# Hybrid encoder block: TensorE's matmuls in the order in which the program traces them

## The chip, the cores and the metric

One core of a Trainium2 chip runs the kernel. The metric is the device time of one execution in microseconds; the time of a kernel is the median of its runs. A separate execution was profiled, and all rows below come from it.

## The reference

One layer on x of 256 tokens by 2048 channels, float32, and a final RMSNorm. Cut to what matters:

```python
def hybrid_layer(x, ...):
    h = rms_norm(x, norm1_g)
    u_a, v_a, feat_b, gate_a, gate_b = split_cols(h @ w_in, ...)
    y_a = sgu_mixer(u_a, v_a, ...)       # gelu, layer norm over channels, 128x128 mix of positions
    y_b = rwkv_mixer(feat_b, ...)        # 16 heads of 64, forward and backward state scans
    merged = sigmoid(gate_a) * (y_a @ w_proj_a) + sigmoid(gate_b) * (y_b @ w_proj_b)
    x = x + merged @ w_out
    h2 = rms_norm(x, norm2_g)
    gt = dwconv3_centred(h2 @ ffn_w_gate, ffn_conv_w, ffn_conv_b)
    return x + (silu(gt) * (h2 @ ffn_w_up)) @ ffn_w_down
```

All weights and activations are float32; w_in has 9,632 columns, the ConvGLU 5,632.

## The kernel before

**Large products.** Every weight column block of 128 is a *job* (`push`, line 196), and its 2048 rows come in *chunks* of four 128x128 blocks. A chunk is loaded by SP (`raw`), split into a high and a low part by a cast on ScalarE (line 271) and a subtraction on VectorE (line 272), and used by TensorE in `advance` (line 276): for each block one matmul of 512 columns with the high part against both parts of the activation (line 294), and one of 256 columns with the low part (line 298). So a chunk has eight matmuls, four pairs. `hl`, the split tiles, has four buffers, and three chunks are split ahead (`HL_AHEAD`). A job's sums are evicted by ScalarE (line 310) and VectorE (line 311). The w_down product at the end uses `tok_mm` (lines 230 to 232).

**Small work between the chunks.** The spatial gating unit (`sgu`, line 470) and the RWKV mixer are Python generators. `run` (line 368) takes a step of a generator, then calls `advance` for as many chunks as the yielded number is worth, and so on. In `sgu` the sum over channels of v is a matmul of `ones` with `acc` (lines 472 and 484), into the PSUM tile ms; then come rsqrt, a transpose (line 497, sgt) and the mix (line 503, sgm).

The RWKV mixer works on eight head pairs p. A round of the loop in line 1011 runs `rwkv_chain(p)` (state steps over four blocks of 64 tokens; matmuls into cc and oc) abreast of `rwkv_inverse(p + 1)` (gp: lines 770 and 782; tp: lines 808 to 859), with `rwkv_rates(p + 2)`. Then, in a second `run`, `rwkv_norm(p)` alternates with `rwkv_operands(p + 2)`. I call this second part the end of the round. Its matmuls all write the pool `ps_ms`, which has one buffer:

- `head_sums` (line 642): two matmuls with `bones`, for the high and the low part `bs` that `split` makes on ScalarE (line 184) and VectorE (line 185);
- the transposes of v (line 731), read by eight ScalarE copies into UV and ZR (lines 739 and 740);
- in `rwkv_norm` the bones of O, read by line 949; the bones of O squared (line 952), read by line 959; and the four g matmuls (lines 965 to 968);
- in `rwkv_operands` the bones of hs (lines 745 and 746), read by line 751.

Round p=-1 has only the inverse of head pair 0; ahead of it the rates and operands of pair 0 run alone. From round p=5 on fewer chunks are left to place between the steps, and round p=6 has no operands, p=7 neither operands nor inverse.

After the rounds come the products with w_pb (activation ybs, after a load sab of spilled gates), w_out (activation mg), the second norm (lines 1099 to 1112) and the ConvGLU.

**The order.** The program is traced in Python order, and a scheduler then orders each engine's queue: an instruction that by its cost table is not ready lets later ones of the same engine pass. So the order on TensorE is not the one in which `advance` and the generators wrote it.

```python
    def head_sums(b):
        ps = ps_ms.tile([P, 512], F32, name="ms", tag="ms")
        for o in range(2):
            PE.matmul(ps[:, 0:T], bones, b[:, o], start=(o == 0), stop=(o == 1))
        return ps[:, 0:T]
```

Of the kernel before, what the change touches and what calls it, by code (L numbers as in the profile page):

```python
# [119 lines left out]
    return out  # L120


@with_exitstack
def hybrid_kernel(ctx: ExitStack, tc: tile.TileContext, xT, w_in, w_pa, w_pb, w_out, w_g, w_u, w_d,
                  cols, consts, lora, sgu_wT, sgu_b, norm_f, out):
    nc = tc.nc
    V, A, PE, G = nc.vector, nc.scalar, nc.tensor, nc.gpsimd

    cpool = ctx.enter_context(tc.tile_pool(name="cpool", bufs=1))
    ps_mm = ctx.enter_context(tc.tile_pool(name="ps_mm", bufs=2, space=PSUM))  # L130
# [880 lines left out]
    for p in range(-1, NP):  # L1011
# [15 lines left out]
        n = left() - (LAST if p == NP - 1 else 0)  # L1027
# [252 lines left out]
```

## Time and profile before

| | us |
|---|---|
| median of three runs | 1546.63 (1545.62 to 1550.25) |
| the profiled execution | 1550.3 |
| its span, first to last instruction | 1548.2 |
| PE busy | 1525.0 (99%) |
| DVE busy | 1214.3 (78%) |
| ACT busy | 925.0 (60%) |
| POOL busy | 38.1 (2%) |

PE is TensorE, DVE VectorE, ACT ScalarE, POOL GpSimd. The 274.65 MB of DMA traffic make 177 GB/s over the span. A matmul's end in the profile is modelled, and matmuls are pipelined, so the distance between the starts of two matmuls says more than their durations.

### The profile page before, as it was taken

The page shows a single profiled execution, that of the slowest core. Times are in us where ns is not written, and L with a number is a line of the kernel's source. Part 1 is how long each engine was busy: PE and PEld are TensorE (multiplying, and loading weights), DVE is VectorE, ACT ScalarE, POOL GpSimd, SP SyncE. Part 2 cuts the span into 40 slices and gives each one's busy share as a digit, 9 for nine tenths or more (in the row PEclk, how much of TensorE's full clock was granted, in tenths as well). Part 3 has the DMA queues.
Part 4 walks back from the last instruction along what each step waited for, and adds up shares of the span by engine and source line. Part 5 has one row for each costly group of instructions (what it writes and reads, how often), then busy time and mean ns, then how long its engine had stood idle before and what let it go on. Part 6 is the DMA issues. An engine that isn't in the chain of part 4 may idle for free.

```text
span 1548.2 us, 34103 instructions
## 1 busy us (share of the span) xinstructions
PE 1525.0 (99%) x12680; PEld 1310.8 (85%) x12680; DVE 1214.3 (78%) x2496; ACT 925.0 (60%) x1946; POOL 38.1 (2%) x63
## 2 busy tenths in 40 slices
PE   9999999999999999989999999999999999999997
PEld 8888888888788878878888888888888888888886
DVE  8979998899889997678778777777777777555544
ACT  7767666665665664556665666665656666544442
POOL 0000000000000000000000000000000000000000
PEclk9999999999999999999999999999999999999999
DMA  8555453443443333587655555555555556766663
GB/s 282 187 176 186 155 165 123 132 133 133 134 141 121 125 100 129 178 272 244 207 189 183 189 191 190 190 189 192 190 190 188 192 188 217 230 193 194 194 175 110
DMA packets 148165, 274.65 MB, mean 177 GB/s; under 512 B 17056, under 2 KB 19232, under 8 KB 147872
## 3 DMA queue, kind: packets, MB, share of 16 engines
q1 hardware_dynamic: 145296, 265.14, 52.7%
q0 software_dynamic: 2560, 7.34, 1.5%
q8 instruction: 99, 1.62, 0.4%
q14 instruction: 66, 0.54, 0.1%
q10 hardware_dynamic: 144, 0.01, 0.0%
HBM read 266.13 MB, written 6.29 MB: 176 GB/s over the span
## 4 chain that ended last, share of the span: by engine, by line
PE 83%; issue 9%; DVE 4%; DMA 1%; ACT 1%; POOL 0%; SPq 0%; DVEq 0%; ACTq 0%; POOLq 0%
PE mm L294 40%; PE mm L298 21%; PE pd L232 5%; PE pd L230 5%; PE pd L231 5%; PE gp L770 1%; PE tp L818 1%; DVE hl L272 1%; PE ms L642 1%; DMA sab<-spill 1%; DVE FQ L796 1%; PE tp L808 1%; DMA spill<-ev 1%; PE cc L901 0%; ACT hl L271 0%
## 5 line engine op out<-in xcount | busy, mean ns | idle before, releaser
L294 PE MATMUL mm<-h,hl 128*128 128x512 f32 x2624 | 930.1, 395 | 0.0
L272 DVE TENSOR_TENSOR hl<-raw,hl 128x512 fp32r<-128x512 f32 x960 | 656.7, 691 | 218.9 <-ACT hl L271 215.5
L271 ACT CAST hl<-raw 128x512 fp32r<-128x512 f32 x960 | 593.5, 621 | 380.3 <-PE mm L298 162.8
L298 PE MATMUL mm<-h,hl 128*128 128x256 f32 x2624 | 740.6, 282 | 1.5 <-DVE hl L272 1.3
L294 PEld LDWEIGHTS mm<-h,hl 128*128 128x128 f32 x2624 | 492.8, 188 | 103.8
L298 PEld LDWEIGHTS mm<-h,hl 128*128 128x128 f32 x2624 | 495.9, 189 | 3.0 <-DVE hl L272 2.1
L310 ACT COPY ev<-mm 128x256 f32<-128x256 f32 x196 | 73.1, 373 | 125.2 <-PE mm L298 123.3
L231 PE MATMUL pd<-hl,act 128*128 128x512 f32 x352 | 136.9, 389 | 0.0
L230 PE MATMUL pd<-hl,act 128*128 128x512 f32 x352 | 136.9, 389 | 0.0
L232 PE MATMUL pd<-hl,act 128*128 128x512 f32 x352 | 136.9, 389 | 0.0
L311 DVE TENSOR_TENSOR ev<-mm,ev 128x256 f32<-128x256 f32 x196 | 82.9, 423 | 44.6 <-ACT ev L310 43.2
L294 PE MATMUL mm<-mg,hl 128*128 128x512 f32 x256 | 90.7, 395 | 0.0
L231 PEld LDWEIGHTS pd<-hl,act 128*128 128x128 f32 x352 | 66.1, 188 | 13.8
L232 PEld LDWEIGHTS pd<-hl,act 128*128 128x128 f32 x352 | 66.1, 188 | 13.8
L230 PEld LDWEIGHTS pd<-hl,act 128*128 128x128 f32 x352 | 66.1, 188 | 13.6
L298 PE MATMUL mm<-mg,hl 128*128 128x256 f32 x256 | 72.1, 282 | 0.0
L294 PEld LDWEIGHTS mm<-mg,hl 128*128 128x128 f32 x256 | 48.1, 188 | 9.6
L294 PE MATMUL mm<-ybs,hl 128*128 128x512 f32 x128 | 46.1, 401 | 4.0 <-DVE ev L311 3.4
L298 PEld LDWEIGHTS mm<-mg,hl 128*128 128x128 f32 x256 | 48.4, 189 | 0.0
L294 PE MATMUL mm<-ya,hl 128*128 128x512 f32 x128 | 47.7, 404 | 0.0
L1161 ACT ACTIVATE gt<-cp,colt 128x256 f32<-128x256 f32 x44 | 26.5, 602 | 19.4 <-DVE cp L1159 19.4
L298 PE MATMUL mm<-ybs,hl 128*128 128x256 f32 x128 | 36.8, 287 | 0.0
(292 smaller groups left out, 1430.5 us busy)
## 6 DMA issues: line engine op xcount, KB each, us to landing
raw<-in_w_in_dram SPq DMA_DIRECT2D x304, 256.0 KB, 2.9
raw<-in_w_g_dram SPq DMA_DIRECT2D x176, 256.0 KB, 2.7
raw<-in_w_u_dram SPq DMA_DIRECT2D x176, 256.0 KB, 2.8
raw<-in_w_d_dram SPq DMA_DIRECT2D x176, 256.0 KB, 3.0
raw<-in_w_out_dram SPq DMA_DIRECT2D x64, 256.0 KB, 3.0
raw<-in_w_pa_dram SPq DMA_DIRECT2D x32, 256.0 KB, 2.9
raw<-in_w_pb_dram SPq DMA_DIRECT2D x32, 256.0 KB, 4.3
spill<-ev POOLq DMA_DIRECT2D x32, 128.0 KB, 3.1
```

Of the source, the lines that this page charges most:

```text
L230: PE.matmul(ps, a[:, 0, ts], w[:, 0], start=(k == 0), stop=False)
L231: PE.matmul(ps, a[:, 0, ts], w[:, 1], start=False, stop=False)
L232: PE.matmul(ps, a[:, 1, ts], w[:, 0], start=False, stop=(k == nk - 1))
L271: A.copy(hl[:, 0, :m], raw[:, s0:s0 + m])
L272: V.tensor_tensor(out=hl[:, 1, :m], in0=raw[:, s0:s0 + m], in1=hl[:, 0, :m].bitcast(F32), op=ALU.subtract)
L294: PE.matmul(ps[:, 0:512], hl[:, 0, j], a.rearrange("p a t -> p (a t)"), start=(k == 0), stop=False)
L298: PE.matmul(ps[:, 0:256], hl[:, 1, j], a[:, 0], start=False, stop=(k == job["nk"] - 1))
L310: A.copy(t, ps[:, 256:512])
L311: V.tensor_tensor(out=t, in0=ps[:, 0:256], in1=t, op=ALU.add)
L642: PE.matmul(ps[:, 0:T], bones, b[:, o], start=(o == 0), stop=(o == 1))
L770: PE.matmul(gps[hh][:, c * P:(c + 1) * P], BK[rows, d, c, hh:hh + 2, :].rearrange("p a b -> p (a b)"), AR[rows, d, c].rearrange("p a b -> ...
L1161: A.activation(gt, b[:, 1:T + 1], AF.Identity, scale=col("cw1", f), bias=col("cb", f))
```

## The change

A wrapper stands in for TensorE's engine object. For each matmul and transpose it adds an edge, without a semaphore, from the previous TensorE instruction. The scheduler thus has to keep TensorE's instructions in traced order, and orders the other engines alone.

```diff
+class InOrder:
+    def __init__(self, tc):
+        self.tc, self.last = tc, None
+
+    def _next(self, op, *args, **kw):
+        tc = self.tc
+        traced = tc.nc.cur_bb.bb.instructions
+        n = len(traced)
+        op(*args, **kw)
+        for ins in traced[n:]:
+            if self.last is not None:
+                tc.add_manual_dep(
+                    ins, self.last.name,
+                    mybir.DependencyInfo(mybir.DependencyClass.NoSync, mybir.DependencyReason.DATA),
+                    reason="order")
+            self.last = ins
+
+    def matmul(self, *args, **kw):
+        self._next(self.tc.nc.tensor.matmul, *args, **kw)
+
+    def transpose(self, *args, **kw):
+        self._next(self.tc.nc.tensor.transpose, *args, **kw)
...
-    V, A, PE, G = nc.vector, nc.scalar, nc.tensor, nc.gpsimd
+    V, A, G = nc.vector, nc.scalar, nc.gpsimd
+    PE = InOrder(tc)
```

All TensorE instructions now carry the wrapper's line 133, and other lines of the kernel stand 27 further down.

What moves, first on TensorE at the end of round p=1. The rows name output, inputs and the size of the output; mm is the sum of a chunk's job, h_ its activations. Before, behind the last eviction of the chain (oc):

```order
L932 MATMUL oc<-Gs,UV 64x64 x4
...
L642 MATMUL ms<-bs,bones 128x256
...
L731 MATMUL ms<-cst,vf 128x128 x4
...
L889 MATMUL cc<-ZR,Gs 64x64 x3
L642 MATMUL ms<-bs,bones 128x256
L889 MATMUL cc<-ZR,Gs 64x64
L770 MATMUL gp<-AR_1690,BK 128x128 x2
L642 MATMUL ms<-bs,bones 128x256
L770 MATMUL gp<-AR_1690,BK 128x128 x5
```

and with the change:

```order
L133 MATMUL mm<-h_99,hl 128x256
L133 MATMUL ms<-bs,bones 128x256 x2
L133 MATMUL ms<-cst,vf 128x128 x4
L133 MATMUL mm<-h_100,hl 128x512
...
L133 MATMUL mm<-h_103,hl 128x256
L133 MATMUL ms<-bs,bones 128x256 x2
L133 MATMUL mm<-h_104,hl 128x512
...
L133 MATMUL ms<-bs,bones 128x256 x2
L133 MATMUL ms<-gsp,lg 128x256 x3
...
L133 MATMUL cc<-ZR,Gs 64x64 x4
L133 MATMUL gp<-AR_1690,BK 128x128 x8
```

Before, the two bones matmuls stand apart with two pairs between them, two more pairs stand ahead of the transposes, and the later bones sit inside the cc and gp matmuls of the next round. Now the bones and the transposes follow each other directly, one chunk stands between each of the later steps, and cc and gp are unbroken.

The same on TensorE at the first sum over acc in `sgu`, before:

```order
L298 MATMUL mm<-h_102,hl 128x256
L472 MATMUL ms<-acc,cst 128x256
L294 MATMUL mm<-h_103,hl 128x512
```

and with the change:

```order
L133 MATMUL mm<-h_111,hl 128x256
L133 MATMUL ms<-acc,cst 128x256
L133 MATMUL mm<-h_96,hl 128x512
```

The sum stood behind the seventh pair (h_102) of the job after the last v job; now it stands directly behind the last pair (h_111) of that v job. The first transpose then follows 16 pairs after the second sum, where 23 and a half stood before.

The third place is on TensorE at the operands of head pair 0, before:

```order
L294 MATMUL mm<-ya_131,hl 128x512
L770 MATMUL gp<-AR_1689,BK 128x128 x3
...
L770 MATMUL gp<-AR_1689,BK 128x128 x4
L642 MATMUL ms<-bs,bones 128x256
L770 MATMUL gp<-AR_1689,BK 128x128
```

and with the change:

```order
L133 MATMUL mm<-ya_130,hl 128x256
L133 MATMUL ms<-bs,bones 128x256 x2
L133 MATMUL mm<-ya_131,hl 128x512
...
L133 MATMUL mm<-ya_134,hl 128x256
L133 MATMUL gp<-AR_1689,BK 128x128 x8
```

The bones matmuls were behind seven of the first eight gp matmuls; now they stand behind four pairs of ya, ahead of all gp matmuls. On POOL and SP no row moves; DVE and ACT have the same instructions with some of them in another order.

## Rows read from the trace of the kernel before

**Rows 1.** The page's busy line: us, share of the span, instructions.
```profile
PE 1525.0 (99%) x12680; PEld 1310.8 (85%) x12680; DVE 1214.3 (78%) x2496; ACT 925.0 (60%) x1946; POOL 38.1 (2%) x63
```
**Rows 2.** Timeline of PE, end of round p=1: start us, us, engine, line, operation, count.
```profile
335.25 0.32 PE L642 MATMUL ms<-bs,bones 128*128 128x256 f32 x1
...
336.99 0.64 PE L731 MATMUL ms<-cst,vf 128*128 128x128 f32 x4
...
340.10 0.44 PE L889 MATMUL cc<-ZR,Gs 64*64 64x64 f32 x6
...
343.59 0.40 PE L294 MATMUL mm<-h,hl 128*128 128x512 f32 x1
...
343.94 0.40 PE L294 MATMUL mm<-h,hl 128*128 128x512 f32 x1
```
**Rows 3.** Busy us by stretch: PE, PEld, DVE, ACT, POOL, clock, DMA share, GB/s.
```profile
150.00:663.00 513.00, 505.29 (x7139) 422.71 (x7137) 445.86 (x1022) 316.90 (x764) 23.77 (x44) 1.00 0.42 137
...
684.00:1540.00 856.00, 854.71 (x4616) 743.43 (x4614) 621.38 (x1153) 487.31 (x924) 10.28 (x8) 1.00 0.61 194
```
**Rows 4.** Waits of PE: waiting line, releaser, total us, times, longest us.
```profile
PE mm L294 <- DVE ev L311: 3.4, 1, 3.4
PE tp L808 <- DVE Tc L800: 3.0, 5, 0.9
...
PE gp L770 <- DVE BK L720: 1.1, 1, 1.1
```
**Rows 5.** Timeline of PE, start of round p=0.
```profile
222.59 0.45 PE L889 MATMUL cc<-ZR,Gs 64*64 64x64 f32 x8
222.97 1.16 PE L770 MATMUL gp<-AR,BK 64*128 64x128 f32 x16
224.06 0.50 PE L294 MATMUL mm<-h,hl 128*128 128x512 f32 x1
```
**Rows 6.** Timeline of all engines, first sum over acc.
```profile
54.94 0.42 DVE L415 TENSOR_TENSOR acc<-acc,vu 128x256 f32<-128x256 f32 x1
...
55.42 0.70 PE L472 MATMUL ms<-acc,cst 128*128 128x256 f32 x2
```
**Rows 7.** Timeline of PE, second sum and first transpose in sgu.
```profile
66.07 0.70 PE L484 MATMUL ms<-acc,cst 128*128 128x256 f32 x2
...
74.97 0.44 PE L497 MATMUL sgt<-cst,vu 128*128 128x128 f32 x2
```
**Rows 8.** Timeline of all engines, operands of head pair 0 (in brackets idle time, releaser).
```profile
166.90 0.40 PE L294 MATMUL mm<-ya,hl 128*128 128x512 f32 x1
...
169.77 0.49 PE L770 MATMUL gp<-AR,BK 64*128 64x128 f32 x2 [1.07 <-DVE BK L720]
...
172.36 0.41 ACT L184 CAST bs<-hs 128x256 fp32r<-128x256 f32 x1
...
172.84 0.41 DVE L185 TENSOR_TENSOR bs<-hs,bs 128x256 fp32r<-128x256 f32 x1
```
**Rows 9.** Timeline of DVE and ACT, end of round p=1.
```profile
335.59 0.42 DVE L185 TENSOR_TENSOR bs<-O,bs 128x256 fp32r<-128x256 f32 x1
...
336.49 0.42 DVE L949 SCALAR_TENSOR_TENSOR O<-ms,O 128x256 f32<-128x256 f32 x1
...
336.96 0.62 ACT L271 CAST hl<-raw 128x512 fp32r<-128x512 f32 x1 [1.11 <-PE mm L298]
...
339.63 0.44 ACT L740 COPY ZR<-ms 128x256 f32<-128x256 f32 x1
```
**Rows 10.** Timeline of PE, end of round p=5.
```profile
561.15 0.73 PE L932 MATMUL oc<-Gs,UV 128*64 128x64 f32 x8 [0.23 <-ACT UV L905]
...
562.96 0.34 PE L642 MATMUL ms<-bs,bones 128*128 128x256 f32 x1
```
**Rows 11.** Timeline of PE and ACT, second norm.
```profile
809.59 0.59 PE L1102 MATMUL ms<-tot,cst 128*128 128x256 f32 x2
...
811.12 0.40 ACT L1099 ACTIVATE sqn<-x 128x256 f32<-128x256 f32 x1
```
**Rows 12.** Busy us by stretch, behind the first sab load (columns as in rows 3).
```profile
680.00:683.30 3.30, 3.30 (x11) 2.82 (x12) 2.69 (x7) 1.17 (x3) 0.00 (x0) 0.52 0.69 222
```

## The prediction

> **What bounds the kernel now.** I read the busy line first. TensorE (PE) is busy 1525.0 us of a span of 1548.2, VectorE (DVE) 78% and ScalarE (ACT) 60% [rows 1]. Busy PE time in this profile is partly modelled, so the pace is what counts: one pair, a 512-column matmul (L294) and its 256-column partner (L298), starts every 0.35 us, 343.59 and 343.94 [rows 2]. I call it a pair, and four pairs (one weight chunk, 1.39 us) a chunk. Then the stretches: from 150 to 663 us, where the RWKV rounds run between the chunks, PE is busy 505.29 of 513.00 us, and from 684 to 1540 us 854.71 of 856.00 [rows 3]. The large stall lies between, at the first sab load; no instruction changes places there, so I leave it as it is. Last the list of PE's waits: three lines make up 7.5 us [rows 4]. So PE is the bound nearly everywhere, and the scheduler has already pushed most small matmuls behind enough chunks that their inputs are ready. There is little waiting left to win. The change can win only in the pace, and it can lose by each wait that the pushed-back chunks hid.
>
> **What the change moves.** No instruction is added or removed. PE's order becomes the traced one; SP and POOL keep their order, and DVE and ACT are reordered a little by a scheduler that now sees PE wait. The kernel traces a small matmul right behind the Python step that makes its input, so at these places PE now arrives early.
>
> *Gain: unbroken runs of small matmuls.* In round p=1 of before, cc and gp matmuls alternate with the bones matmuls of `head_sums`. From the first cc to the next chunk it takes 343.59 - 340.10 = 3.49 us [rows 2]. The same cc and gp groups in one piece took 224.06 - 222.59 = 1.47 us [rows 5]. Four bones matmuls of 256 columns in the stream cost a third of a pair each (0.48 together), so 1.54 us went into four interruptions, 0.39 each. The traced order has none. Rounds p=0 to 4 have about four each (in p=0, 2, 4 one of them is gp split by a chunk), and round p=-1 four: 24 x 0.4 = **-9.6 us**.
>
> *Loss 1, SGU.* The first sum over acc (L472) is traced right behind the last chunk of v; before, seven pairs stand ahead of it that now stand behind. PE would come at 55.42 - 7 x 0.345 = 53.0 us, and the last addition to acc ends at 54.94 + 0.42 = 55.36 [rows 6]: a wait of 2.4. From the second sum (66.07) to the first transpose sgt (74.97) it takes 8.9 us through the rsqrt chain [rows 7]; PE now has only 16 pairs in between, 0.34 + 5.5 = 5.9. On DVE and ACT one eviction and one cast leave the path (about 0.9), so I take 2.1. **+4.5 us**, bounds 2.4 and 5.4.
>
> *Loss 2, first operands.* The bones matmuls of p=0 move ahead of gp, after only four pairs of ya: PE comes at 166.90 + 1.4 = 168.3. Their two input halves start on ACT at 172.36 and on DVE at 172.84 [rows 8]. One eviction less stands ahead on each, so I take 172.2 and 172.7 for the matmuls: 3.9 + 0.4 of waiting, against the 1.07 that PE waits there before [rows 4, 8]. **+3.2 us**; the bounds are 1.5 (two split tiles leave the path) and 4.2 (nothing does).
>
> *Loss 3, the end of each round,* where `rwkv_norm` and the next `rwkv_operands` alternate on the single ms buffer. I go through p=1, with one chunk between steps. (a) bones: the second half comes from DVE at 335.59 + 0.42 = 336.01, so the second bones matmul cannot start before 336.1; the first starts at 335.25, and the 0.73 between was filled with two pairs. (b) The v transposes (L731) now follow at once, but the ms buffer must first be read by L949, 336.49 to 336.91: 0.7. (c) The bones of the squares need ms again, which eight ACT copies read until 339.63 + 0.44 = 340.07, 3.1 us after the transposes start at 336.99; PE has the transposes and one chunk, 1.85: 1.2. (d) The next bones wait 0.25 for DVE, and the g matmuls (L965) 0.9 for L751, which reads ms behind two other DVE tiles. Sum 3.8, and before waits nowhere here [rows 2, 9]. Rounds p=1 and p=3 are alike: 7.6. Rounds p=0, 2, 4 have two chunks at (c), so (c) falls away, and (a) is 0.35; 1.75 less the 0.46 waited now, 1.3 each: 3.9. Round p=5 has no chunk ahead of (a): from L932 at 561.15 PE comes at about 561.6 and bones can start at 562.96 [rows 10]: 1.3, 0.3, 0.9, 1.85, 0.1, 0.7 less about 0.9 waited now: 4.2. Round p=6 has no operands: 0.6 + 0.3 + 0.7 = 1.6. Round p=7 is in the traced order already. **+17.3 us**; the lower bound is 9, if in each wait one split tile of 0.69 us leaves the chain, the upper 21, if L949 and L751 queue behind one more.
>
> *Loss 4, the rest.* At the second norm the sum over sqn now stands ahead of the chunks: its input is ready at 811.12 + 0.40, and PE comes about 1.4 earlier, right after the first half (L1102) [rows 11]; with 0.2 at the end of p=-1 **+1.6 us**.
>
> *A wait that shrinks.* DVE now places the predicated copies of one direction ahead of the second direction's evictions. Of the 3.0 us for Tc [rows 4] I take back **-0.7** (bounds 0 and -1.4).
>
> What is queued behind a waiting PE: the chunks, whose split tiles wait for a free hl buffer; ACT's casts already wait for PE, and nothing else waits for them. As PE is the bound, each wait goes to the end of the kernel undiminished.
>
> **The clock.** The wait of 3.4 us at the first sab load [rows 4] ended at 680.0 us, and from there to 683.30 the granted clock was 0.52, the lower of its two levels (1.2 GHz) for nearly all of the stretch [rows 12]: 3.3 x (1 - 0.52) = 1.6 us lost. The waits of 1.1 us and less were followed by none, since the clock is 1.00 from 150 to 663 us [rows 3]. Loss 2 with its 3.9 us is the only new wait of such length, and chunks stand close on both sides; I price it at nothing, with 1.6 as its upper end. The Trainium skill ("TensorE: Matmul & The Clock Gate", section on the HAM clock gate) has the throttled state as the default, which activity releases. By that rule loss 2, and perhaps the row of waits in p=5, would each add the 1.6 us; by the rows of the short waits neither would.
>
> **The sum.** -9.6 + 4.5 + 3.2 + 17.3 + 1.6 - 0.7 = +16.3 us. The profiled execution took 1550.3 us (span 1548.2 and 2.1 around it), 3.7 more than the median of 1546.63; on the median the forecast is 1546.6 + 16.3 = **1563 us**, 1.1% slower. A measurement can tell about 0.3%, 4.6 us, from no change.
>
> **Rivals.**
> *The waits are half as long* (same). DVE and ACT have fewer split tiles to do while PE stands, and the scheduler now puts norm and operands ahead of them. With loss 3 at 8.6 and losses 1 and 2 at 4: -9.6 + 8.6 + 4 + 1.6 - 0.7 = +3.9, 1550.5. For it: ACT's next cast of p=1 starts only when PE frees a buffer [rows 9]. Against: (b) and the g matmuls wait for one DVE instruction that starts at once already, and (c) for eight copies in a row. 0.11.
> *The pace wins* (faster). Place: the ends of the rounds. If the reordered chains are ready there when PE comes, loss 3 is nothing, with losses 1 and 2 at half: -9.6 - 0.7 + 1.6 + 3.9 = -4.8, 1542. It decides from the point where all new waits together stay below 5.7 us. Against it stands the single ms buffer, which no order on DVE or ACT removes. 0.07.
> *The clock falls* after loss 2 and in p=5: +3.2, 1566. For it speaks the one long wait of before, against it every short one [rows 3, 4, 12]. 0.12.
> *The waits feed on each other:* DVE and ACT tiles queued behind splits that wait for PE, as ACT's cast does for 1.11 us in p=1 [rows 9]; the upper bounds of losses 1 to 3 add 0.9 + 1.0 + 3.7, with the clock 3.2: 1572. Against it: three chunks are split ahead (HL_AHEAD). 0.08.
> *The change does not do what it says:* excluded, since the built program has PE in the traced order.
>
> **How the numbers follow.** The forecast has 0.62. Slower by over 0.3% are the forecast, the clock and the queues: 0.62 + 0.12 + 0.08 = 0.82; same 0.11; faster 0.07. The forecast's own bounds are all lower ends, 1563 - 2.1 - 1.7 - 8.3 = 1551, and 1569 at the upper. For 8 in 10 the range takes in the upper part of the rival with no change and the last rival: 1549 to 1574.
>
> **What would show it.** Right: in the list of PE's waits, lines for the bones, transposes and g matmuls behind DVE and ACT, together some 20 us more, and gaps of about 2.4, 2 and 4 us near 53, 73 and 168 us; cc and gp in one piece in every round. Wrong: rounds p=1 and p=3 not longer than before, or the time from 684 us on differing by more than 2 us.

## The result and the profile after

| | us |
|---|---|
| median before, same chip (4 runs) | 1546.12 (1545.16 to 1550.25) |
| median after (4 runs) | 1565.2 (1564.48 to 1565.66) |
| ratio | 1.0118, 95% interval 1.0099 to 1.0137 |
| profiled execution after, its span | 1565.35, 1563.6 |

The change costs 19.1 us; the forecast was 1563. The busy line of the page after, against [rows 1]:

```profile
PE 1519.9 (97%) x12680; PEld 1306.0 (84%) x12680; DVE 1215.7 (78%) x2496; ACT 925.2 (59%) x1946; POOL 38.1 (2%) x63
```

The same work on every engine: DVE and ACT within 1.4 us of before, PE even 5 us less, in a longer span. So the time went into PE standing still. By stretch (columns as in [rows 3]; the first row against the first one there, the second stands behind the operands of pair 0, the last behind the first sum over acc):

```profile
150.00:676.00 526.00, 502.91 (x7148) 420.73 (x7147) 450.88 (x1028) 319.81 (x770) 23.77 (x44) 1.00 0.41 134
178.20:181.70 3.50, 3.50 (x19) 2.82 (x19) 2.92 (x8) 2.63 (x6) 0.00 (x0) 0.51 0.75 257
55.50:60.00 4.50, 3.60 (x20) 3.19 (x21) 3.67 (x10) 2.24 (x7) 0.00 (x0) 1.00 0.40 131
```

From the operands of pair 0 to the end of the rounds PE is now idle for 526.00 - 502.91 = 23.1 us, where it was 7.7. Who makes it wait is in the list of PE's waits (columns as in [rows 4]):

```profile
PE ms L133 <- ACT bs L211: 5.0, 3, 3.8
PE ms L133 <- DVE bv L778: 4.5, 6, 1.0
PE ms L133 <- ACT ZR L767: 3.4, 3, 1.3
PE ms L133 <- DVE O L976: 3.1, 6, 0.6
PE mm L133 <- DVE ev L338: 2.6, 1, 2.6
PE ms L133 <- DVE acc L442: 2.6, 1, 2.6
PE sgt L133 <- ACT vu L521: 1.9, 1, 1.9
PE ms L133 <- DVE tmp L986: 1.7, 4, 0.7
...
PE ms L133 <- ACT sqn L1126: 1.4, 1, 1.4
```

Of these rows only that of ev (the first sab load) stood in [rows 4]; the others are small matmuls that now arrive before their input or their buffer. The rows of Tc and BK (L800 and L720 there) are gone from the list. The timeline shows four of the places: the first sum over acc [rows 6], the first transpose [rows 7], the operands of pair 0 [rows 8], and the end of round p=1 [rows 2]:

```profile
56.40 0.70 PE L133 MATMUL ms<-acc,cst 128*128 128x256 f32 x2 [2.59 <-DVE acc L442]
...
76.08 0.44 PE L133 MATMUL sgt<-cst,vu 128*128 128x128 f32 x2 [1.90 <-ACT vu L521]
...
177.34 0.89 PE L133 MATMUL ms<-bs,bones 128*128 128x256 f32 x2 [3.76 <-ACT bs L211]
...
342.30 0.38 PE L133 MATMUL ms<-bs,bones 128*128 128x256 f32 x1
343.17 0.38 PE L133 MATMUL ms<-bs,bones 128*128 128x256 f32 x1 [0.49 <-DVE bs L212]
344.07 0.66 PE L133 MATMUL ms<-cst,vf 128*128 128x128 f32 x4 [0.52 <-DVE O L976]
344.48 1.64 PE L133 MATMUL mm<-h,hl 128*128 128x512 f32 x8
347.15 0.51 PE L133 MATMUL ms<-bs,bones 128*128 128x256 f32 x2 [1.03 <-ACT ZR L767]
...
350.49 0.62 PE L133 MATMUL ms<-gsp,lg 128*128 128x256 f32 x3 [0.99 <-DVE bv L778]
```

Each place has a releaser on DVE or ACT in brackets, while whole chunks (the mm row of eight) stand behind it and then run without a wait of their own. Where along the kernel the time goes shows in the starts of the same matmul in three profiles: us from the start in the first profile of before, and the difference to it in the second profile of before (below) and in the changed kernel:

| start of | before | before again | after |
|---|---|---|---|
| second transpose of the SGU | 77.23 | -0.06 | +5.14 |
| last gp matmul of pair 0's first stage (AR, BK) | 179.67 | -0.08 | +7.75 |
| last matmul of the last round's gate | 651.71 | +0.26 | +17.79 |
| last matmul on ybs (w_pb) | 717.55 | -2.70 | +13.88 |
| first matmul of w_d | 1299.18 | -2.68 | +15.38 |

### The profile page after: what moved, and what is told of

It is laid out like the page before. It is cut to its first block, busy times and chain, and to the rows that moved or that the text cites. A ratio compares the mean times of both kernels' runs of the same rounds, so it can differ in the third digit from the quotient of the medians.

```text
span 1563.6 us, 34129 instructions
## 1 busy us (share of the span) xinstructions
PE 1519.9 (97%) x12680; PEld 1306.0 (84%) x12680; DVE 1215.7 (78%) x2496; ACT 925.2 (59%) x1946; POOL 38.1 (2%) x63
## 4 chain that ended last, share of the span: by engine, by line
PE 63%; DVE 4%; ACT 2%; issue 1%; DMA 1%; DVEq 0%; SPq 0%; ACTq 0%
PE mm L133 45%; PE pd L133 15%; DVE hl L299 1%; PE tp L133 1%; PE cc L133 1%; DMA sab<-spill 1%; PE ms L133 0%; ACT hl L298 0%; ACT Gs L896 0%; PE gp L133 0%; DVE FQ L823 0%; PE oc L133 0%; DVE ev L338 0%; DVE Gs L800 0%; PE xt L133 0%
## 5 line engine op out<-in xcount | busy, mean ns | idle before, releaser
L133 PE MATMUL mm<-h,hl 128*128 128x512 f32 (+1 forms) x5248 | 947.5, 338 | 0.4 <-DVE hl L299 0.2
L133 PEld LDWEIGHTS mm<-h,hl 128*128 128x128 f32 x5248 | 805.6, 188 | 106.2 <-DVE hl L299 0.5
L133 PE MATMUL pd<-hl,act 128*128 128x512 f32 x1056 | 239.5, 389 | 0.0
L133 PE MATMUL mm<-mg,hl 128*128 128x512 f32 (+1 forms) x512 | 92.1, 338 | 0.0
L133 PEld LDWEIGHTS mm<-mg,hl 128*128 128x128 f32 x512 | 78.6, 188 | 9.6
L133 PE MATMUL mm<-ya,hl 128*128 128x512 f32 (+1 forms) x256 | 51.8, 347 | 0.0
L133 PE MATMUL mm<-ybs,hl 128*128 128x512 f32 (+1 forms) x256 | 44.9, 337 | 3.2 <-DVE ev L338 2.6
L133 PEld LDWEIGHTS mm<-ybs,hl 128*128 128x128 f32 x256 | 39.3, 188 | 8.7 <-ACT ev L337 2.9
L133 PEld LDWEIGHTS mm<-ya,hl 128*128 128x128 f32 x256 | 39.9, 191 | 5.2
L1005 POOL DMA_DIRECT2D spill<-ev x32 | 17.3, 541 | 425.4 <-ACT ev L1010 188.3
L133 PEld LDWEIGHTS ms<-bs,bones 128*128 128x128 f32 x64 | 10.6, 187 | 18.8 <-ACT bs L211 7.3
L211 ACT CAST act<-ev 128x256 fp32r<-128x256 f32 x44 | 17.9, 407 | 10.9 <-DVE ev L1199 10.9
L1189 DVE SCALAR_TENSOR_TENSOR gt<-cp,colt,gt 128x256 f32<-128x256 f32 x44 | 21.3, 485 | 3.2
L1190 DVE SCALAR_TENSOR_TENSOR gt<-cp,colt,gt 128x256 f32<-128x256 f32 x44 | 21.4, 486 | 1.6
```

The source lines that it names most:

```text
L133: op(*args, **kw)
L211: A.copy(dst[:, 0], src)
L1005: G.dma_start(spill[m][:, o], t)
L1189: V.scalar_tensor_tensor(out=gt, in0=b[:, 0:T], scalar=col("cw0", f), in1=gt, op0=ALU.mult, op1=ALU.add)
L1190: V.scalar_tensor_tensor(out=gt, in0=b[:, 2:T + 2], scalar=col("cw2", f), in1=gt, op0=ALU.mult, op1=ALU.add)
```

## The experiments

Medians of several runs, beside 1546.5 to 1547.4 us for before in the same sessions.

**Before, profiled again.** No edit.

> The kernel before, unchanged, profiled once more. The profiled execution of before took 1550.3 us, 3 to 4 more than the median. Theory: those stand at the first sab load (a wait of 3.4 us by the list of waits, and a clock of 0.52 behind it): this time the wait is under 3 us, no stretch at 0.52 follows, and up to 650 us every place stands within 1 us of the first profile; span about 1544 us. Rival: they are spread over the rounds, and the sab load waits as long as before.

1547.62 us in the one execution profiled, span 1545.5. The table shows it: up to 652 us within 0.3 us of the first profile, then 3 us shorter up to the last matmul on ybs. From the list of waits and a window behind the load:

```profile
PE mm L294 <- DVE ev L311: 2.1, 1, 2.1
```
```profile
678.40:681.90 3.50, 3.50 (x13) 3.00 (x12) 2.62 (x6) 1.04 (x3) 0.00 (x0) 0.53 0.83 259
```

The wait was shorter, as expected; that the clock would not fall was wrong: 0.53 over 3.5 us, about as long as in the first profile [rows 12]. The 3 us are thus the shorter wait for ev (2.1 for 3.4 us) and a wait of 1.3 us for a split tile at 663 us that is down to 0.2 here. So of the 3.9 us that the changed kernel seems to win there, 3 are what the first profile of before happened to lose.

**The order in the SGU alone.**

```diff
     run([(sgu(), 22.0)], SGU_CHUNKS)
     finish(last_lo)
+    PE.on = False
```

(`PE.on` switches the edges off for what is traced later.)

> TensorE follows the trace only until the last low-rank feature has been issued (the normalization of the SGU and its transposes); after that the scheduler orders it, as before. Theory (a small matmul that waits holds back the chunk matmuls traced behind it, place by place): the changed kernel is 5.1 us behind at the second transpose of the SGU, of it 2.75 us before the first sum over acc and 2.12 us before the first transpose, and nothing later gives that back. So 1551 us (1549.5 to 1552.5) against 1546.1 before, with those two waits and no others of the changed kernel. Rival (the stages behind have waits of their own that take up a late SGU): 1546 to 1548 us, with the two waits still there.

1551.88 us, ratio 1.0033 (1.0021 to 1.0045): 4.7 us. The shift of 4.4 us at the second transpose stays between 4.4 and 4.6 up to 656 us. Nothing behind takes it up.

**The ends of the rounds free.**

```diff
         run(side, n0)
+        PE.on = False
         run(then, n - n0)
+        PE.on = True
```

> TensorE follows the trace everywhere but in the end of each round, where norm and operands run; there the scheduler may move chunks ahead again. Theory: what goes are the waits at the ends of the rounds, 19.8 us in the changed profile by place (1.95 three times, 3.8 twice, 4.65, 1.65), and what comes back are the chunks broken up by small matmuls, 9.8 us (the rounds cost 10.0 us on balance): 1555 us (1553 to 1557). Rival A (the order of the other engines has moved with TensorE's, and the rounds are longer whether the ends are free or not): 1562 to 1566 us. Rival B (the broken chunks were in the middle of the rounds, not at their ends, so that freeing the ends takes the waits and gives nothing back): 1545 to 1549 us.

1563.17 us, ratio 1.0098 (1.0085 to 1.0111): a miss. From the last oc of a round to the next round's first gp it now takes 9.7 us (p=0, 2, 4) or 7.7 (p=1, 3), as before; the changed kernel took 12.0 or 12.4. But the middles, from there to the last oc, grew: p=1 and p=3 from 48.0 to 50 us, p=2 and p=4 from 49.7 to 52.5. And p=5 won nothing (11.1 for 10.4). The chunks did not move: 5 or 4 of them stand in an end and 22 or 23 in a middle, in both kernels. The small matmuls did. What is traced with the edges off may slide behind the next round's first matmuls, and the later bones and g matmuls do, as in the kernel before. The start of the middle of p=2:

```profile
348.46 0.44 PE L133 MATMUL cc<-ZR,Gs 64*64 64x64 f32 x6
348.83 0.39 PE L133 MATMUL ms<-bs,bones 128*128 128x256 f32 x1
349.15 0.32 PE L133 MATMUL cc<-ZR,Gs 64*64 64x64 f32 x2
...
351.73 0.38 PE L133 MATMUL ms<-bs,bones 128*128 128x256 f32 x1
```

In the changed kernel these cc and gp take 1.47 us; here, from 348.46 to 351.73, 3.27, the same as in the kernel before. Less the 0.12 us of each small matmul in between, the breaks cost 1.43 or 1.44 us at the start of each of the middles of p=1 to 5, 7.2 us in all, in this kernel as in the one before. Two rows of its waits show what else came:

```profile
PE tp L133 <- DVE Tc L827: 3.5, 5, 1.1
PE ms L133 <- ACT ZR L767: 2.5, 1, 2.5
```

The waits for Tc, which the changed kernel has not, are back. The second row is one wait in the end of p=5; the 4.65 us of waits that the theory took off there stayed, and the clock behind them was 0.52 from 578.9 to 585.9 us, 3.4 us lost. Over the rounds 6.2 us are lost instead of 10.0. Another 0.9 us went in the SGU: behind the wait for acc the clock fell (0.62 from 55.5 to 60 us), which it did not in the changed kernel (the window above, 1.00). So waits do go and interruptions do come back, as the theory had it; what it missed is p=5 and the clock. The time lies in rival A's range, but not by its mechanism.

**Two chains.** The chunks in traced order among themselves, the small matmuls among themselves.

```diff
-            if self.last is not None:
+            if self.kind in self.lasts:
...
-                    ins, self.last.name,
+                    ins, self.lasts[self.kind].name,
...
+            PE.kind = "chunk"
             for j in range(m):
```

> Two orders in place of one: the small matmuls keep the traced order among themselves, the chunk matmuls among themselves, and the scheduler may again put a chunk ahead of a small matmul that waits. Theory (the loss is chunks held back behind waiting small matmuls): nearly all of the 19 us go, 1546 us (1543 to 1549), and the wait of 2.75 us at the first sum of the SGU and that of 3.9 us in the operands of pair 0 are no longer in the trace. Rival (it is the fixed order of the small matmuls among themselves that costs, since one that is late holds up others that are ready): the waits stay, 1557 to 1565 us.

1544.1 us (12 runs), ratio 0.998 (0.997 to 0.999): as the theory had it, and 3 us better than before, a difference of 0.2% that the interval only just sets apart from none. The same end of p=1 in its timeline:

```profile
333.94 0.34 PE L135 MATMUL ms<-bs,bones 128*128 128x256 f32 x1
334.12 0.86 PE L135 MATMUL mm<-h,hl 128*128 128x256 f32 x4
334.81 0.34 PE L135 MATMUL ms<-bs,bones 128*128 128x256 f32 x1
334.99 0.86 PE L135 MATMUL mm<-h,hl 128*128 128x256 f32 x4
335.68 0.64 PE L135 MATMUL ms<-cst,vf 128*128 128x128 f32 x4
336.08 3.03 PE L135 MATMUL mm<-h,hl 128*128 128x256 f32 x16
339.13 0.39 PE L135 MATMUL ms<-bs,bones 128*128 128x256 f32 x1
```

The small ones stand in traced order, with four chunk matmuls where the changed kernel waited 0.49 us, four where it waited 0.52, and sixteen where it had eight and waited 1.03; no row has a wait in brackets. The order of the small matmuls costs nothing; that chunks may not pass them does.

**Two buffers for ms.**

```diff
-        vps = ps_ms.tile([P, 512], F32, name="ms", tag="ms")
+        vps = ps_g.tile([P, 512], F32, name="gp", tag="gp")
...
-        gp2 = ps_ms.tile([P, 512], F32, name="ms", tag="ms")
+        gp2 = ps_g.tile([P, 512], F32, name="gp", tag="gp")
```

> The changed kernel, with two results of the rounds' ends (the transposed values of the operands, and the gate of the norm) in the pool of two PSUM buffers instead of the single buffer ms that all head sums share. Theory (of the waits at the rounds' ends, the second, third and last are for the one buffer, read by VectorE and ScalarE): they go, 1.55 us in each of three rounds, 2.73 in each of two, 3.0 and 0.7 in the last two: 13.8 us, so 1551.5 us (1550 to 1556). Rival (the operands of these matmuls are late as well, and the buffer is only the later of the two by the profile): under 4 us go, 1561 to 1565 us.

1603.65 us, ratio 1.0365 (1.0345 to 1.0384): 38 us slower still than the changed kernel, which neither side expected. From its waits, and its timeline behind p=1:

```profile
PE gp L133 <- DVE yb L996: 24.4, 6, 4.8
PE ms L133 <- ACT bs L211: 14.1, 9, 3.8
```
```profile
364.47 0.48 PE L133 MATMUL gp<-AR,BK 64*128 64x128 f32 x2
...
367.81 2.07 PE L133 MATMUL gp<-AR,BK 64*128 64x128 f32 x14 [2.86 <-DVE yb L996]
```

The gate's matmul now comes early, but its result is read only at yb, behind the rsqrt of the norm. Until then it holds one of the two gp buffers, and the next round's first gp, directly behind it in the fixed order, needs both. In ms nothing needed the buffer so soon. The waits are only part of the price: the rows of its list add up to 55.0 us, 22.5 more than in the changed kernel, where the profiled span is 43.9 longer. The clock is 0.979 over the whole execution, 0.997 in the changed kernel, with stretches of 3.5 to 7 us near the lower level behind the waits for yb and for bs.

**Two idle buffers instead** (`ps_c`, tag cc, for vps; `ps_t`, tag tp, for gp2).

> The changed kernel, with the transposed values in the PSUM buffer of the chain (cc) and the gate of the norm in that of the inverse (tp), both idle at the end of a round, where the run before put them into the pair that the next round's inverse needs first. Theory A (the second and last waits of each round's end are for the single buffer ms): 0.5 us in each of six rounds and 0.6, 1.1, 1.0 or 0.7 in seven go, 8.8 us, 1557 us or less. Theory B (the chain of small VectorE and ScalarE steps sets the length of a round's end, and a wait that is taken away comes back at the next head sum; in the run with two buffers the head sums of the squares in round p=1 waited 2.19 us for ScalarE where the changed kernel waits 1.14): about 0.5 us a round go, 1562 us (1560 to 1565), and the head sum of the squares waits about 2 us in p=1 and p=3.

1568.38 us, ratio 1.0136 (1.0119 to 1.0154): theory A falls; B has the longer head sum right, and its half microsecond shows where the clock stays up: from the last oc to the next gp 0.46 us go in p=0, 2 and 4. The waits for O, ZR and bv are gone from the list, but bs L211 again has 14.1 us in nine. ACT's timeline in p=1 tells why, first the changed kernel, then this one:

```profile
344.05 0.42 ACT L979 ACTIVATE tmp<-O 128x256 f32<-128x256 f32 x1 [1.09 <-DVE O L976]
...
344.81 0.36 ACT L766 COPY UV<-ms 128x256 f32<-128x256 f32 x1
```
```profile
344.95 0.37 ACT L766 COPY UV<-cc 128x256 f32<-128x256 f32 x1 [1.08 <-PE cc L133]
...
347.06 0.50 ACT L979 ACTIVATE tmp<-O 128x256 f32<-128x256 f32 x1
...
348.41 0.39 PE L133 MATMUL ms<-bs,bones 128*128 128x256 f32 x1 [2.11 <-ACT bs L211]
```

In the changed kernel the squares (L979) ran ahead of the eight copies of vps, and the head sum then waited 1.03 us for its buffer until the copies were through. With a buffer of its own vps is there earlier, so ACT takes the eight copies first, and the head sum waits 2.11 us for the squares, which stand behind them. The eight copies lie on the path of p=1 either way; the buffer only named them. (The copies behind the squares with a free buffer, by an order on ACT, were not tried.) Behind such waits the next chunk also ran at the lower clock level: 1.7 us were lost to it in p=1 (0.51 from 349.6 to 353.1), as much in p=3, and 3.4 in p=5. The ends of p=1 and p=3 are 1.05 us longer than in the changed kernel. Over the rounds this kernel is 2.4 us longer than the changed one, with 6.8 us lost to the clock; so the run shows that the waits came back under other names, not what a free buffer alone is worth.

**More chunks in the ends.**

```diff
-BY = 1.0
+BY = 1.8
```

> The changed kernel with BY at 1.8 for 1.0: of the chunks of each round 7 or so stand in its end, where 4 or 5 stood, and as many fewer in its middle. Theory (the steps of norm and operands take their time on VectorE and ScalarE, and chunks between the head sums cover it): the waits at the ends, 19.8 us, fall to under 10, and the middles have room: 1556 us (1553 to 1559). Rival (the middle needs its chunks: the chain and the inverse wait for their own evictions there): the waits of cc, uc and tp grow by what the ends win, 1562 to 1570 us.

1557.38 us, ratio 1.0073 (1.0058 to 1.0088): 8 us back with one number, near the middle of what the theory gave. The rounds now cost 4.2 us against before (10.67 at the end of the last less 6.44 ahead of the first), where they cost 10.0. The idle time of PE in their ends fell from 15.1 to 9.8 us; in p=0, 2 and 4 it rose a little (1.84 each for 1.39), although eight chunks stand there instead of five.

**Chunks at the three other places.**

```diff
     def sgu():
+        yield 1.5
...
         rsqrt(rs, sv, tv)
-        yield 1
+        yield 2
...
         bp = parts(ks)
-        yield SY
+        yield SY + (3 if p == 0 else 0)
...
-    fin2()
     advance(2)
+    fin2()
```

(with the second norm's sums moved into `fin2`, SGU_CHUNKS at 48, and the totals of the two runs raised to match)

> The changed kernel with chunks traced where TensorE waits outside the rounds: three ahead of the first sum over acc, two more behind the rsqrt of the SGU, three more ahead of the head sum in the operands of pair 0, and the second norm's sums behind the two chunks that stood behind them. Theory (each of these waits is only for lack of a chunk ahead of it): 2.75, 2.1, 3.9 and 1.5 us go, and with the wait of 3.9 us the 1.7 us at a clock of 0.54 behind it, 11 to 12 us: 1554.5 us (1552.5 to 1557). Rival (the chunks taken are missed later: the rates of pair 0 wait, and the chunks that come earlier stall on their own splits): half of it comes back, 1559 to 1562 us.

1558.07 us, ratio 1.0069 (1.0055 to 1.0083): some 7 of the 11 to 12 us. Up to the last gp of pair 0 it stands 1.14 us behind before, where the changed kernel stood 7.75, and the second norm's 1.5 are gone; the rival has the rest, by two rows that are new in the list or have grown (hl had 0.2):

```profile
PE mm L133 <- DVE hl L299: 2.6, 2, 2.4
...
PE ms L133 <- DVE acc L508: 1.1, 1, 1.1
```

The three chunks for the operands came out of the rates of pair 0, and there a chunk waits 2.4 us for its split on DVE. Behind it the clock was 0.53 from 168.6 to 172.1 us, so the 1.7 us at the lower clock, which the theory took off, stayed too.

**All weights together** (BY 1.8, the three places, FILLS beginning with 2 and ending with 6).

> The changed kernel with the chunks of both runs before put where TensorE waits: at the three places outside the rounds (and four more chunks in the operands of pair 0, taken from the last round, since the run before waited 2.4 us there for a chunk's split), and BY at 1.8. Theory (the waits are independent, each gone once a chunk stands ahead of it): 8 us of the run with BY and 10 of the run with the three places come off the 19: 1548 us (1545 to 1551), level with before. Rival (VectorE is the next bound: a chunk moved ahead brings its split with it, which queues with the steps that the head sum waits for): 1552 to 1557 us, with waits of chunks for hl in the list.

1547.81 us (11 runs), ratio 1.0003 (0.9994 to 1.0011): level with before. Both gains are there, and the fixed order is as good as the scheduler's once the trace has the chunks where they are needed.

**Two chains, and more chunks ahead of Tc** (the yield behind Tc at 2.6 for 1.2).

> The two chains, with more chunks traced between the steps of the inverse and its first use of Tc (2.6 for 1.2 in its yield). In the run of two chains the largest waits left in the rounds are for Tc, 3.7 us in six, since chunks that stood there were moved ahead to the ends of the rounds. Theory: they fall under 1.5 us and nothing takes their place: 2 to 3 us less than the two chains, 1541.5 us (1539 to 1543.5) where before takes 1546.5. Rival (the scheduler moves these chunks ahead as well): no change, 1543 to 1546 us.

1545.55 us, ratio 0.9989 (0.998 to 0.9998): no gain on the two chains, whose ratio of 0.998 has an overlapping interval. The waits for Tc went from 3.7 us in six to 2.8 in four, and 1.1 us for a chunk's cast is new.

**What an interruption costs.** 32 matmuls in front of cc and gp, then the same 32 inside.

```diff
+    def extra(n):
+        if n:
+            ps = ps_t.tile([P, 512], F32, name="tp", tag="tp")
+        for _ in range(n):
+            PE.matmul(ps[:, 0:T], bones, gsp[:, 0], start=True, stop=True)
```

> The changed kernel with 32 matmuls more, of the size of a head sum's (128x256), whose result nobody reads: in rounds 0 to 6 four in one piece ahead of cc, three ahead of gp in the round before, one ahead of cc in the last. They measure, with the next run, what an interruption costs (0.39 us each by the prediction). Theory: only their own 0.11 to 0.12 us each, 3.7 us: 1569 us (1567.5 to 1571) where the changed kernel takes 1565 to 1566. Rival (they cover waits of the next round, or the switch to them costs as well): 1565 to 1567 or over 1572 us.

1567.68 us, ratio 1.0130 (1.0116 to 1.0144), inside the theory's range: a round is 0.46 to 0.48 us longer than in the changed kernel, 0.12 for each.

> The same 32 matmuls, each inside the cc or gp matmuls: one in the middle of the four cc, one behind the second, fourth and sixth of the eight gp. Theory (an interruption costs 0.39 us): 32 x 0.39 = 12.5 us more than with the matmuls in one piece, about 1581.5 us (1578 to 1585). Rival (the interruptions of before were short waits, not switches, and a switch between such matmuls costs little): 1569 to 1573 us, within 4 us of the run in one piece.

1583.87 us, ratio 1.0241 (1.0217 to 1.0264), again as the theory had it. The timelines at the start of round p=1, first in one piece, then inside:

```profile
293.04 0.64 PE L133 MATMUL tp<-gsp,bones 128*128 128x256 f32 x4
293.61 0.45 PE L133 MATMUL cc<-ZR,Gs 64*64 64x64 f32 x8
293.99 1.16 PE L133 MATMUL gp<-AR,BK 64*128 64x128 f32 x16
295.08 4.43 PE L133 MATMUL mm<-h,hl 128*128 128x512 f32 x24
```
```profile
300.77 0.33 PE L133 MATMUL cc<-ZR,Gs 64*64 64x64 f32 x4
301.04 0.38 PE L133 MATMUL tp<-gsp,bones 128*128 128x256 f32 x1
301.35 0.33 PE L133 MATMUL cc<-ZR,Gs 64*64 64x64 f32 x4
301.61 0.49 PE L133 MATMUL gp<-AR,BK 64*128 64x128 f32 x4
...
304.24 4.43 PE L133 MATMUL mm<-h,hl 128*128 128x512 f32 x24
```

3.47 us (304.24 - 300.77) against 2.04 (295.08 - 293.04) for the same matmuls, with no wait in brackets: 1.43 for four, 0.36 each. By the starts of the last gp a round is 1.52 us longer, 0.38 each. Seven rounds at 1.52 make 10.6 us; the rest of the medians' 16.2 comes from the operands of pair 0, where the last gp starts 6.1 us later and the interrupted gp run into the slow clock (below). The Trainium skill ("TensorEngine Tiling (Array Packing)", section on key properties) says that a change of the tiling mode, not of the tile alone, drains TensorE; with sums over 128 rows between matmuls on 64, the 0.36 to 0.38 us here agree with it. Between chunk matmuls, which are on 128 rows too, such a sum can take as little as its own 0.12 us: in the kernel before one starts at 275.15 and the next chunk matmul at 275.27. A break by a matmul on 64 rows was not tried, so that the tile shape is the reason is argued, not shown.

## Why the prediction was right

By place, the terms of the text against the differences to the second profile of before (span 1563.6 - 1545.5 = 18.1 us):

| | predicted | measured |
|---|---|---|
| SGU | 4.5 | 5.2 |
| operands of pair 0 (3.2, less four interruptions 1.6) | 1.6 | 2.6 |
| rounds (17.3 + 0.2, less 20 interruptions 8.0 and Tc 0.7) | 8.8 | 9.7 |
| sab load | 0 | -0.9 |
| second norm | 1.4 | 1.5 |

- **Gain, unbroken runs (-9.6).** The price is confirmed by the pair of runs, 0.36 to 0.38. In the rounds the text had 20 x 0.4 = 8.0; before loses 7.2 there (1.43 or 1.44 at five starts of cc and gp, by three breaks inside them rather than four) and the changed kernel nothing.
- **Tc (-0.7, bounds 0 and -1.4)** was too small: all 3.0 us of L800 in [rows 4] are gone. The rounds p=0 to 7 lost 19.8 us in waits at their ends (by the distance between starts; the idle times in brackets add up to 15.1) and 10.0 on balance; 7.2 and 3.0 nearly account for the 9.8 that came back.
- **Loss 1 (+4.5)** measured 2.59 and 1.90 us of waiting and a shift of 5.1; alone, the order in the SGU costs 4.7.
- **Loss 2 (+3.2).** PE waits 3.76 us for ACT and then starts the second half 0.50 behind the first, where the text had 3.9 and 0.4 of waiting. The clock behind it was priced at nothing, and that step failed: 0.51 from 178.2 to 181.7, 3.5 x 0.49 = 1.7 us, more than the 1.0 us that the place costs beyond the text.
- **Loss 3 (+17.3)** measured 19.8. (a) 0.75, (b) 0.53, (c) 1.14 and (d) 1.27 in p=1 and p=3 make 3.7, for 3.8; p=6 1.65 for 1.6. In p=0, 2, 4 it is 1.95 each and in p=5 4.65, where the text has 1.75 and 5.1 before it takes off what the kernel before waits there (0.46 three times and 0.9). So the waits are sized well, 19.8 for 19.6; the 2.3 taken off are what is wrong. The list of before has one such wait, in p=5:

```profile
PE ms L642 <- ACT ZR L740: 0.5, 1, 0.5
```

  That (c) falls away with two chunks in front holds: in p=0 the bones of the squares start 0.12 us behind the second chunk's last matmul, and the waits there are (a), (b) and (d). That (c) waits for eight ACT copies holds too. That the single ms buffer is what has to go is not borne out: with idle buffers the same head sums of p=1 and p=3 wait longer, for their input, and the ends of p=0, 2 and 4 gain 0.46 each.
- **The total.** In the rounds the waits cost 2.5 us more than the text has, Tc gave 2.3 more back and the pace 0.8 less: together about the 0.9 by which the rounds cost more. That the sum came so close is in part luck, since two of these errors cancel.
- **The sab load**, which the text left as it was, varies by 3 us between the two profiles of before. The changed kernel waits 2.6 us there and no lower clock follows, where 1.7 us were lost to it in both of those.
- **The rivals.** Half as long waits, and the pace winning: not in the changed kernel; the two chains have the unbroken cc and gp (1.47 us in every round) without these waits, and gain 3 us. Of the clock's rival half came true, behind loss 2 and not in p=5. That waits feed on each other does not show in the changed kernel, whose waits at the ends are the 19.6 of the text within 0.2.

What the ends of the rounds need was argued from single waits, and the run with free ends shows that this sum cannot be taken apart stretch by stretch: small matmuls that are let go in one stretch break the matmuls of the next. Why the end of p=5 kept its waits there stays open.

## What to carry to other kernels

A fixed order on the bounding engine costs each wait that a ready instruction could have filled; fix the order within the independent kinds of work (here the bulk and the small matmuls) and leave their merge free, or give the trace bulk work ahead of each late step. Before a buffer is blamed for a wait, ask when its producer's input is ready and who needs the new buffer next. Keep small matmuls of one tile shape in one piece: in this kernel each sum of another shape between them cost 0.36 us or more. And price the clock behind a new wait of some microseconds: here it cost 1.7 us behind a single wait, and in the runs with other buffers it hid what the buffer did.

## What was not expected of the hardware

The granted clock did not follow the length of a wait alone. Behind the wait for acc the window from 55.5 to 60 us shows 1.00 in the changed kernel, after 2.6 us of waiting, and 1.00 after 2.8 with the 32 matmuls inside; but 0.62 in the runs with free ends, with two gp buffers and with idle buffers, after 2.3 us each, and again 1.00 after 2.3 us with the order in the SGU alone. Behind the wait of 3.8 us in the operands of pair 0 it fell to the lower level (1.2 GHz) in all of these that have this wait, but not for equally long: 3.5 us in the changed kernel, 7 us with two gp buffers (0.51 from 179.2 to 186.2), although the same matmuls follow there in the same order, and 12.5 us with the gp matmuls interrupted:

```profile
178.50:191.00 12.50, 12.12 (x42) 9.03 (x43) 8.27 (x19) 3.67 (x8) 0.54 (x1) 0.50 0.44 140
```

PE counts as busy there all the same, with 42 matmul records in 12.5 us. What decides whether and for how long the clock falls stays open here.
